# Shifting the start addresses of matmul operands inside their tiles in a hybrid mLSTM, neighbourhood and memory attention block

## The chip, the cores and the metric

The kernel runs on one core of one Trainium2 chip. The metric is the device time of one execution in microseconds (us), as the median of several runs; lower is better. Beside the runs there is one profiled execution, whose trace gives the start and length of every instruction.

## The reference

One encoder block for 512 tokens of width 1024, all in float32:

```python
h = rms_norm(x, mix_norm_g[l])
proj = h @ w_in[l]        # mLSTM q,k,v,o,gates | NA q,k,v | memory q | merge gates
y_ml = mlstm_branch(...)             # 4 heads of 128, both directions
y_na = neighbourhood_attention(...)  # 8 heads of 64 on an 8 x 64 grid
mem_k, mem_v = jnp.split(rms_norm(mem, mem_norm_g[l]) @ w_mem_kv[l], 2, axis=-1)
y_xa = memory_cross_attention(xa_q, mem_k, mem_v)   # 256 memory tokens
merged = g_ml * (y_ml @ w_br_ml[l]) + g_na * (y_na @ w_br_na[l]) + g_xa * (y_xa @ w_br_xa[l])
x = x + merged @ w_out[l]
x = x + conv_glu_ffn(rms_norm(x, ffn_norm_g[l]), ...)   # 1024 -> 2 x 2816 -> 1024
return rms_norm(x, final_norm_g)
```

Almost all of the arithmetic is in the dense projections: `w_in`, `w_mem_kv`, the three branch projections, `w_out`, and the two matrices of the feed-forward part.

## The kernel before

**Products in three parts.** To keep float32 accuracy with single-pass matmuls, both operands are split into a high part (the value rounded to the type fp32r) and a low part (what is left). The helper `mm3` (line 212) issues three matmuls for each 128-deep slice: high times high (line 213), high of the first with low of the second (line 214), low of the first with high of the second (line 215). In all of them the first operand is the stationary one, loaded into the array ahead of the matmul (a row of engine PEld, LDWEIGHTS), and the second is the moving one, which streams through it (a row of engine PE, MATMUL).

**Weights as a queue of blocks.** `block_list` writes out the order of all weight blocks, and `BLOCKS` is that order. A block's key names its kind: `mlq`, `mlk` (mLSTM queries and keys), `tm` (token-major passes: gates, values and the values of the neighbourhood attention, in three passes c = 0, 1, 2 of 272, 512 and 256 columns), `xaq`, `o`, `memk`, `memv`, `naq`, `nak`, `g` (merge gates), `br` (branch projections), `out`, `ua` and `uu` (the two halves of the feed-forward's first matrix), `dn` and `dnl` (its second matrix; `dn` has a first half, hh = 0, and a second, hh = 1; `dnl` belongs to the last two column blocks). `weights(key)` (line 201) keeps the transfers three blocks ahead (`emit_raw`, SyncE's queue, tile `wr`) and the splitting one block ahead (`emit_split`, line 176). `emit_split` cuts a block into at most two parts, and for each takes a tile `wh` (tag hi) and a tile `wl` (tag lo), each `HWT` = 576 words wide, four buffers of each: ScalarE copies the raw weights into `wh` (line 195), and VectorE subtracts to give `wl` (line 196).

**Where operands start.** A word is 4 bytes. `wh`, `wl`, the big working tiles (`unit`, 2112 words), the scratch tiles (512 words) and the raw tiles (1088 words) are all a multiple of 256 bytes long, and slices of 128, 256 or 512 words keep that phase. The constant `HI256` = 48 words (192 bytes) is the one exception of the kernel before: it shifts `wh` of the third token-major pass (lines 188 and 189), and the high part of the weights of the last column blocks, which `lastw` (line 169) keeps in four units; their low parts are not shifted.

**Which operand is which.** In projections (`proj`, line 395) the weights are stationary and the activations, 512 tokens (or 256 for the memory), are moving. In the token-major passes and for `memv` the activations are stationary and the weights moving. In `last_tiles` (line 1159) `half_tile` does the last three column blocks over the first 256 tokens, the first of them (key `dn`) over the second 256 as well, with stationary weights; after that the last two blocks are done for two groups of 128 tokens with moving weights, 256 columns.

**The attentions.** While TensorE works through projections, steps of the mLSTM and of the two attentions are put between them by generators (`step`, line 998). They share four tiles of tag R (512 words each): the rows of the mLSTM's decays (`load_R`, line 646), the queries and keys of the neighbourhood attention (`QS`, `KS`, lines 808 and 809), and queries, keys and values of the memory attention (`rt`, line 920). The neighbourhood attention's keys are the moving operand of lines 834 and 835, read as eight rows of 32 words in windows that start 0, 8, 24 or 32 words into the row (`CW`). Its gathered values lie in a unit filled by DMA (`load_vwin`, line 531) and are the stationary operand of line 872.

Of the kernel before, what the change touches and what calls it, by code (L numbers as in the profile page):

```python
# [11 lines left out]
F32 = mybir.dt.float32  # L12
F32R = mybir.dt.float32r
# [4 lines left out]
P = 128  # L18
S = 512
# [14 lines left out]
BW = 1088  # L34

GAP = 16

HI256 = 48
HWD, HWT = 544, 576
UNIT = 2112  # L40
ROWS, GW = 8, 64
# [69 lines left out]
def hybrid_block(ctx, tc, xg, xT, memT, wflat, vecs, gbias, nabias, outa, outb, outc):  # L111
# [7 lines left out]
    tp = ctx.enter_context(tc.tile_pool(name="tp", bufs=2))  # L119
# [6 lines left out]
    def nm(s):  # L126
        uid[0] += 1
        return f"{s}_{uid[0]}"

    def unit(dt=F32):  # L130
        return up.tile([P, UNIT], dt, tag="unit", name=nm("u"))
# [4 lines left out]
    def tiny(n):  # L136
        return tp.tile([P, 32], F32, tag="tiny", name=nm("y"), bufs=12)[:, :n]

    def mmps():
        return mmp.tile([P, 512], F32, tag="mm", name=nm("mm"))  # L140

# [19 lines left out]
    def halves(i):  # L161
        n, c = BLOCKS[i][1], BCOLS[BLOCKS[i][0][0]](BLOCKS[i][0])
        k = n // c
        k0 = k if n <= HWD else (k + 1) // 2
        return c, [(0, k0)] + ([(k0, k)] if k0 < k else [])

    lw = []

    def lastw(k, m):

        if not lw:
            lw.extend(unit(F32R) for _ in range(4))
        q = slice(k % 8 * 256, k % 8 * 256 + m)
        return lw[k // 8][:, HI256:][:, q], lw[2 + k // 8][:, q]

    def emit_split(i):
        key, n = BLOCKS[i]
        r = raws.pop(i)
        c, hs = halves(i)
        split[i] = []  # L180
        for a, b in hs:
            m = (b - a) * c
            if key[0] == "dnl":
                h, l = lastw(4 * key[1] + a, m)
            else:
                h = wp.tile([P, HWT], F32R, tag="hi", name=nm("wh"), bufs=4)
                l = wp.tile([P, HWT], F32R, tag="lo", name=nm("wl"), bufs=4)
                if key[:2] == ("tm", 2):
                    h = h[:, HI256:]
            for u, v in ((0, P), (P, 2 * P), (2 * P, m)) if i == 0 and a == 0 else ((0, m),):  # L190
                src = r[:, a * c + u:a * c + v]
                if i == 0 and u == 0:
                    st["wh1"] = V.tensor_copy(h[:, u:v], src).ins
                else:
                    A.activation(h[:, u:v], src, AF.Copy)  # L195
                V.tensor_tensor(l[:, u:v], src, h[:, u:v].bitcast(F32), op=ALU.subtract)  # L196
            for k in range(a, b):
                q = slice((k - a) * c, (k - a + 1) * c)
                split[i].append((h[:, q], l[:, q]))
# [17 lines left out]
    def split_act(h, l, src, scale=1.0):  # L217

        A.activation(h, src, AF.Copy, scale=scale)  # L219
        V.scalar_tensor_tensor(l, src, scale, h.bitcast(F32), op0=ALU.mult, op1=ALU.subtract)  # L220
# [48 lines left out]

    cp.tile([P, GAP], F32, name="gap")  # L270
    ident = cp.tile([P, P], F32, name="ident")
# [16 lines left out]
    for i in range(2):  # L288
        t = cp.tile([P, 514], F32, name=f"pad{i}")
# [210 lines left out]
    for c in range(3):  # L500
# [10 lines left out]
        for t in range(NT):  # L511
# [3 lines left out]
            if c < 2:  # L515
                o = 16 if c == 0 else 0
# [13 lines left out]

    def load_vwin(hp):

        vw = unit(F32R)
        for b in range(4):
            for hf in range(2):
                i = 2 * b + hf
                for r in range(4):
                    G.dma_start(vw[r * 32:(r + 1) * 32, i * 256:(i + 1) * 256],  # L538
                                nav_v[hf, r, CW[b]:CW[b] + 32, hp * 256:(hp + 1) * 256])
        return vw  # L540
# [101 lines left out]
    def ml_all():  # L642
# [3 lines left out]
        def load_R(h):  # L646
            R, rm = [], []
            for d in range(2):
                t = tp.tile([P, S], F32, tag="R", name=nm("R"), bufs=4)
                SY.dma_start(t, rd[d, h].partition_broadcast(P))  # L650
                R.append(t)
                rm.append(tp.tile([P, S], F32, tag="R", name=nm("R"), bufs=4))
            return R, rm

        def mask(R, rm):
# [105 lines left out]
        R, rm = load_R(0)  # L761
        st_h = keys(0)
        yield
        for h in range(4):
# [11 lines left out]
            for J in range(1, NT):  # L776
                E2 = weights_J(h, J, R, rm)
                if J == 3 and h < 3:
                    R, rm = load_R(h + 1)
# [14 lines left out]
    def na_all(nq, nk, vw0, yh, yl):  # L794
# [6 lines left out]
        def prep(hp):  # L801
            qn = nq[:, hp * S:(hp + 1) * S]
            kn = nk[:, hp * S:(hp + 1) * S]
            QL = QZ[hp % 2]
            QS, KS = [], []
            for e in range(2):
                own, oth = slice(64 * e, 64 * e + 64), slice(64 - 64 * e, 128 - 64 * e)
                q2 = tp.tile([P, S], F32R, tag="R", name=nm("QS"), bufs=4)
                k2 = tp.tile([P, S], F32R, tag="R", name=nm("KS"), bufs=4)
                A.activation(q2[own], qn[own], AF.Copy)  # L810
                A.activation(k2[own], kn[own], AF.Copy)
                A.activation(q2[oth], qn[own], AF.Copy)
                V.tensor_tensor(k2[oth], kn[own], k2[own].bitcast(F32), op=ALU.subtract)
                V.tensor_tensor(QL[e][own], qn[own], q2[own].bitcast(F32), op=ALU.subtract)
                QS.append(q2)
                KS.append(k2.rearrange("p (r w) -> p r w", r=ROWS))
            return QS, KS, QL
# [99 lines left out]


    def xa_all(xq, mk, mv, yh, yl):
        rt = lambda: tp.tile([P, S], F32R, tag="R", name=nm("X"), bufs=4)  # L920
        vv = lambda a: a.rearrange("p (m c) -> p m c", m=2)

        def prep(h):
            q, k = (rt(), rt()), rt()
            split_act(q[0], q[1], xq[:, h * S:(h + 1) * S])
            k = (k[:, :M], k[:, M:])
            split_act(k[0], k[1], mk[:, h * M:(h + 1) * M])
            return q, k

        def prep_v(h):  # L930
            v = rt()
            v = (v[:, :M], v[:, M:])
            split_act(vv(v[0]), vv(v[1]), vv(mv)[:, :, h * P:(h + 1) * P])
            return v

        def scores(tq, q, k):
            ps = atps()
            for i in range(2):
                t = 2 * tq + i
                tsl = slice(t * P, (t + 1) * P)  # L940
                mm3(ps[:, i * M:(i + 1) * M], q[0][:, tsl], q[1][:, tsl], k[0], k[1], True, True)
            mx = tiny(2)
            psv = ps.rearrange("p (a b) -> p a b", a=2)
            V.tensor_reduce(mx, psv, axis=AX.X, op=ALU.max, negate=True)
            V.tensor_scalar(mx, mx, XSC, None, op0=ALU.mult)
            sm = scr()
            su = tiny(2)
            for i in range(2):
                A.activation(sm[:, i * M:(i + 1) * M], psv[:, i, :], AF.Exp, scale=XSC, bias=mx[:, i:i + 1],
                             accum_out=su[:, i:i + 1])  # L950
            V.reciprocal(su, su)
            for i in range(2):
                V.tensor_scalar(sm[:, i * M:(i + 1) * M], sm[:, i * M:(i + 1) * M], su[:, i:i + 1], None, op0=ALU.mult)
            return sm

        def transposes(tq, sm, pT):
            pt = atps()
            for i in range(2):
                for hf in range(2):
                    PE.transpose(pt[:, (2 * hf + i) * P:(2 * hf + i + 1) * P],  # L960
                                 sm[:, i * M + hf * P:i * M + (hf + 1) * P], ident)
            for hf in range(2):
                ms = slice(tq * M, (tq + 1) * M)
                split_act(pT[hf][0][:, ms], pT[hf][1][:, ms], pt[:, hf * M:(hf + 1) * M])

        def values(h, v, pT):
            py = atps()
            for hf in range(2):
                vs = slice(hf * P, (hf + 1) * P)
                mm3(py, v[0][:, vs], v[1][:, vs], pT[hf][0], pT[hf][1], hf == 0, hf == 1)  # L970
            hs = slice(h * S, (h + 1) * S)
            split_act(yh[:, hs], yl[:, hs], py)

        q, k = prep(0)
        yield
        prev = None
        for h in range(4):
            sm = [scores(tq, q, k) for tq in range(2)]
            if prev:
                values(h - 1, *prev)  # L980
            yield
            v = prep_v(h)
            pT = [[sp.tile([P, S], F32R, tag="scr", name=nm("s"))[:, :S] for _ in range(2)] for _ in range(2)]
            for tq in range(2):
                transposes(tq, sm[tq], pT)
            prev = (v, pT)
            if h < 3:
                q, k = prep(h + 1)
            yield
        values(3, *prev)  # L990
        yield
# [28 lines left out]
    for f in range(4):  # L1020
# [5 lines left out]
        t = scr()  # L1026
# [262 lines left out]
    for hh in range(2):  # L1289
# [3 lines left out]
        for j in range(HF):  # L1293
            f = HF * hh + j
            if f == 0:
# [7 lines left out]
                k = KT - 1  # L1303
# [150 lines left out]
```

## Time and profile before

| | us |
|---|---|
| median of 3 runs (lowest, highest) | 879.12 (878.70, 879.23) |
| profiled execution, span from first to last instruction | 878.1 |
| TensorE matmul busy in it | 872.7 |
| TensorE weight load busy | 740.4 |
| VectorE busy | 582.2 |
| ScalarE busy | 451.4 |
| GpSimd busy | 127.1 |

The profile's page gives, for each engine, the time in which it was busy. A matmul counts as busy from its start to its modelled end, and successive matmuls overlap, so that a busy share near 100% says that there was always one under way, not how fast they follow each other. The time from one start to the next, here called the gap, is read from the timeline, or from the windows view: a stretch that begins and ends at starts of matmuls, divided by the number of gaps in it. Weight loads (PEld) run beside matmuls. The groups view lists the instructions of a line with their operands, written out<-in by the names of the tiles, their shape and count, busy time and mean length.

### The profile page before, as it was taken

To read this page: it belongs to the slowest core of one execution; us is meant where nothing else is said; L and a number is where in the kernel's file an instruction comes from. 1 tells how busy PE (TensorE), PEld (TensorE's weight loads), DVE (VectorE), ACT (ScalarE), POOL (GpSimd) and SP (SyncE) were. 2 spreads that over 40 slices of the span, in tenths; PEclk is the share of its full clock that TensorE was granted. 3 is DMA by queue.
4 is the path that set the end of the run, shared out by engine and by line. 5 is a ranking of instruction groups with operands and counts; after the bars stand their busy time and mean duration, and the time that the engine had idled before them with its cause. 6 is when DMAs were issued, how large, how long until landed. Compare 5 with 4: busy or idle time off the path is not lost.

```text
span 878.1 us, 12238 instructions
## 1 busy us (share of the span) xinstructions
PE 872.7 (99%) x4334; PEld 740.4 (84%) x4334; DVE 582.2 (66%) x1211; ACT 451.4 (51%) x953; POOL 127.1 (14%) x203
## 2 busy tenths in 40 slices
PE   9999999999999999999999999999999999999997
PEld 7898889888888888888888888888888888888897
DVE  7694686775667758898676558776633466666433
ACT  7363555754456658888544435444422344444532
POOL 0101100001072460700000002111100011111011
PEclk9999999999999999999999999999999999999999
DMA  8224643522242354533223432222233322222412
GB/s 280 99 73 140 207 135 97 192 85 90 74 137 87 107 146 131 156 110 130 97 97 109 144 107 94 99 97 96 72 103 101 109 97 97 98 97 87 141 34 96
DMA packets 39421, 99.81 MB, mean 114 GB/s; under 512 B 5688, under 2 KB 13880, under 8 KB 39360
## 3 DMA queue, kind: packets, MB, share of 16 engines
q1 hardware_dynamic: 31568, 92.32, 31.1%
q0 software_dynamic: 7360, 6.32, 3.1%
q8 instruction: 34, 0.56, 0.3%
q10 hardware_dynamic: 432, 0.39, 0.1%
q14 instruction: 27, 0.22, 0.1%
HBM read 94.80 MB, written 4.21 MB: 113 GB/s over the span
## 4 chain that ended last, share of the span: by engine, by line
PE 99%; issue 0%; ACT 0%; DVE 0%; POOLq 0%; POOL 0%; DVEq 0%
PE mm L213 29%; PE mm L215 29%; PE mm L214 29%; PE at L214 2%; PE at L213 2%; PE at L215 2%; PE at L872 1%; PE at L725 1%; PE at L853 1%; PE at L727 1%; PE at L690 1%; PE at L834 0%; PE at L835 0%; PE at L706 0%; PE at L960 0%
## 5 line engine op out<-in xcount | busy, mean ns | idle before, releaser
L213 PE MATMUL mm<-u,wh 128*128 128x512 f32 (+1 forms) x1072 | 415.6, 388 | 0.0
L215 PE MATMUL mm<-u,wl 128*128 128x512 f32 (+1 forms) x1072 | 412.2, 385 | 0.0
L214 PE MATMUL mm<-u,wh 128*128 128x512 f32 (+1 forms) x1072 | 411.8, 384 | 0.0
L195 ACT ACTIVATE wh<-wr 128x512 fp32r<-128x512 f32 (+2 forms) x298 | 184.1, 622 | 234.4 <-PE mm L214 188.1
L196 DVE TENSOR_TENSOR wl<-wr,wh 128x512 fp32r<-128x512 f32 (+3 forms) x300 | 203.1, 678 | 92.4 <-ACT wh L195 85.8
L215 PEld LDWEIGHTS mm<-u,wl 128*128 128x128 f32 x1072 | 201.5, 188 | 40.1
L214 PEld LDWEIGHTS mm<-u,wh 128*128 128x128 f32 x1072 | 201.8, 188 | 38.8
L213 PEld LDWEIGHTS mm<-u,wh 128*128 128x128 f32 x1072 | 201.8, 188 | 38.2
L1319 POOL TENSOR_TENSOR s<-s,rb 128x512 f32<-128x512 f32 x22 | 38.3, 1739 | 250.0 <-DVE s L1318 238.1
L538 POOL DMA_DIRECT2D u<-nav_d x128 | 62.2, 512 | 66.5 <-PE at L872 22.5
L219 ACT ACTIVATE u<-s 128x512 fp32r<-128x512 f32 x26 | 16.4, 630 | 57.5 <-DVE s L1322 56.1
L1322 DVE TENSOR_TENSOR s<-mm,s 128x512 f32<-128x512 f32 x22 | 15.2, 691 | 25.1 <-POOL s L1319 25.1
L458 ACT ACTIVATE s<-pad,vec 128x512 f32<-128x512 f32 x30 | 24.4, 813 | 9.5 <-DVE pad L456 9.5
L459 DVE SCALAR_TENSOR_TENSOR s<-pad,vec,s 128x512 f32<-128x512 f32 x30 | 23.6, 786 | 6.1 <-ACT s L458 6.0
L220 DVE SCALAR_TENSOR_TENSOR u<-s,u 128x512 fp32r<-128x512 f32 x26 | 18.0, 691 | 14.1 <-ACT u L219 14.0
L1318 DVE SCALAR_TENSOR_TENSOR s<-s,s 128x512 f32<-128x512 f32 x22 | 15.2, 692 | 13.4 <-ACT s L1317 13.3
L317 POOL TENSOR_TENSOR rc<-y,nhalf 128x4 f32<-128x4 f32 x1 | 1.0, 1032 | 152.9 <-DVE y L314 152.9
L460 DVE SCALAR_TENSOR_TENSOR s<-pad,vec,s 128x512 f32<-128x512 f32 x30 | 22.5, 750 | 0.7
L1317 ACT ACTIVATE s<-s 128x512 f32<-128x512 f32 x22 | 13.9, 632 | 15.1 <-DVE s L1316 15.1
L456 DVE TENSOR_TENSOR pad<-mm,rb 128x512 f32<-128x512 f32 x22 | 15.1, 691 | 7.3 <-PE mm L215 6.5
L213 PE MATMUL mm<-wh,u 128*128 128x512 f32 x48 | 18.9, 394 | 0.0
L214 PE MATMUL mm<-wl,u 128*128 128x512 f32 x48 | 18.8, 392 | 0.0
(315 smaller groups left out, 1028.4 us busy)
## 6 DMA issues: line engine op xcount, KB each, us to landing
wr<-wflat SPq DMA_DIRECT2D x141, 512.0 KB, 3.3
nab<-nabias SPq DMA_DIRECT2D x16, 256.0 KB, 2.7
u<-nav_d POOLq DMA_DIRECT2D x128, 32.0 KB, 2.6
s<-xT SPq DMA_DIRECT2D x15, 256.0 KB, 3.9
wr<-wflat SPq DMA_DIRECT2D x14, 192.0 KB, 2.3
nav_d<-nv POOLq DMA_DIRECT2D x8, 256.0 KB, 2.4
R<-rd SPq DMA_DIRECT2D x8, 256.0 KB, 3.9
wr<-wflat SPq DMA_DIRECT2D x2, 544.0 KB, 3.3
```

The lines of the kernel that those rows point to most:

```text
L195: A.activation(h[:, u:v], src, AF.Copy)
L196: V.tensor_tensor(l[:, u:v], src, h[:, u:v].bitcast(F32), op=ALU.subtract)
L213: PE.matmul(ps, lh, rh, start=start, stop=False)
L214: PE.matmul(ps, lh, rl, start=False, stop=False)
L215: st["mm"] = PE.matmul(ps, ll, rh, start=False, stop=stop).ins
L219: A.activation(h, src, AF.Copy, scale=scale)
L220: V.scalar_tensor_tensor(l, src, scale, h.bitcast(F32), op0=ALU.mult, op1=ALU.subtract)
L458: A.activation(t1, pad[:, 0:512], AF.Identity, scale=vcol(w, i), bias=vcol(b, i))
L459: V.scalar_tensor_tensor(t1, pad[:, 1:513], vcol(w, n + i), t1, op0=ALU.mult, op1=ALU.add)
L460: V.scalar_tensor_tensor(t1, pad[:, 2:514], vcol(w, 2 * n + i), t1, op0=ALU.mult, op1=ALU.add)
L538: G.dma_start(vw[r * 32:(r + 1) * 32, i * 256:(i + 1) * 256], nav_v[hf, r, CW[b]:CW[b] + 32, hp * 256:(hp + 1) * 256])
L1319: G.tensor_tensor(c, c, rb2, op=ALU.mult)
```

## The change

The weights' high and low tiles are both read and written from a start inside the tile, by kind of block: 16 words (64 bytes) for `ua`, `out`, `xaq` and `mlk`; 32 words (128 bytes) for `g`, `br`, `memv`, `naq`, all token-major passes and the second half's `dn`; 48 words (192 bytes) for `uu`, `o`, `memk` and `nak`; none for `mlq` and the first half's `dn`. The third token-major pass, where only the high part had 192 bytes, has 128 for both. The last column blocks' low parts get the 192 bytes that the high parts have. The gathered values start 192 bytes into their unit. The tag R tiles grow from 512 to 576 words, and the keys of both attentions start 64 bytes into theirs. No instruction is added or removed.

```diff
--- before.py
+++ after.py
@@ -34,8 +34,11 @@
 BW = 1088
 
 GAP = 16
+KOFF = 16
 
 HI256 = 48
+OFFSETS = {"ua": 16, "uu": 48, "g": 32, "br": 32, "out": 16, "xaq": 16, "o": 48, "memk": 48, "memv": 32,
+           "naq": 32, "nak": 48, "mlk": 16, "mlq": 0, "dn": 0}
 HWD, HWT = 544, 576
 UNIT = 2112
 ROWS, GW = 8, 64
@@ -136,6 +139,9 @@
     def tiny(n):
         return tp.tile([P, 32], F32, tag="tiny", name=nm("y"), bufs=12)[:, :n]
 
+    def rtile(dt=F32, off=0):
+        return tp.tile([P, S + 64], dt, tag="R", name=nm("R"), bufs=4)[:, off:off + S]
+
     def mmps():
         return mmp.tile([P, 512], F32, tag="mm", name=nm("mm"))
 
@@ -171,7 +177,7 @@
         if not lw:
             lw.extend(unit(F32R) for _ in range(4))
         q = slice(k % 8 * 256, k % 8 * 256 + m)
-        return lw[k // 8][:, HI256:][:, q], lw[2 + k // 8][:, q]
+        return lw[k // 8][:, HI256:][:, q], lw[2 + k // 8][:, HI256:][:, q]
 
     def emit_split(i):
         key, n = BLOCKS[i]
@@ -185,8 +191,10 @@
             else:
                 h = wp.tile([P, HWT], F32R, tag="hi", name=nm("wh"), bufs=4)
                 l = wp.tile([P, HWT], F32R, tag="lo", name=nm("wl"), bufs=4)
-                if key[:2] == ("tm", 2):
-                    h = h[:, HI256:]
+                off = 32 if key[0] == "tm" else OFFSETS[key[0]]
+                if key[:2] == ("dn", 1):
+                    off = 32
+                h, l = h[:, off:], l[:, off:]
             for u, v in ((0, P), (P, 2 * P), (2 * P, m)) if i == 0 and a == 0 else ((0, m),):
                 src = r[:, a * c + u:a * c + v]
                 if i == 0 and u == 0:
@@ -530,7 +538,7 @@
 
     def load_vwin(hp):
 
-        vw = unit(F32R)
+        vw = unit(F32R)[:, HI256:]
         for b in range(4):
             for hf in range(2):
                 i = 2 * b + hf
@@ -646,10 +654,10 @@
         def load_R(h):
             R, rm = [], []
             for d in range(2):
-                t = tp.tile([P, S], F32, tag="R", name=nm("R"), bufs=4)
+                t = rtile()
                 SY.dma_start(t, rd[d, h].partition_broadcast(P))
                 R.append(t)
-                rm.append(tp.tile([P, S], F32, tag="R", name=nm("R"), bufs=4))
+                rm.append(rtile())
             return R, rm
 
         def mask(R, rm):
@@ -805,8 +813,8 @@
             QS, KS = [], []
             for e in range(2):
                 own, oth = slice(64 * e, 64 * e + 64), slice(64 - 64 * e, 128 - 64 * e)
-                q2 = tp.tile([P, S], F32R, tag="R", name=nm("QS"), bufs=4)
-                k2 = tp.tile([P, S], F32R, tag="R", name=nm("KS"), bufs=4)
+                q2 = rtile(F32R)
+                k2 = rtile(F32R, KOFF)
                 A.activation(q2[own], qn[own], AF.Copy)
                 A.activation(k2[own], kn[own], AF.Copy)
                 A.activation(q2[oth], qn[own], AF.Copy)
@@ -917,18 +925,17 @@
 
 
     def xa_all(xq, mk, mv, yh, yl):
-        rt = lambda: tp.tile([P, S], F32R, tag="R", name=nm("X"), bufs=4)
         vv = lambda a: a.rearrange("p (m c) -> p m c", m=2)
 
         def prep(h):
-            q, k = (rt(), rt()), rt()
+            q, k = (rtile(F32R), rtile(F32R)), rtile(F32R, KOFF)
             split_act(q[0], q[1], xq[:, h * S:(h + 1) * S])
             k = (k[:, :M], k[:, M:])
             split_act(k[0], k[1], mk[:, h * M:(h + 1) * M])
             return q, k
 
         def prep_v(h):
-            v = rt()
+            v = rtile(F32R)
             v = (v[:, :M], v[:, M:])
             split_act(vv(v[0]), vv(v[1]), vv(mv)[:, :, h * P:(h + 1) * P])
             return v
```

## The prediction

> **What bounds the kernel now.** I read the page's busy times and slices first, to see whether any other engine could set the end.
>
> ```profile
> span 878.1 us, 12238 instructions
> ...
> PE 872.7 (99%) x4334; PEld 740.4 (84%) x4334; DVE 582.2 (66%) x1211; ACT 451.4 (51%) x953; POOL 127.1 (14%) x203
> ...
> PEclk9999999999999999999999999999999999999999
> ...
> PE 99%; issue 0%; ACT 0%; DVE 0%; POOLq 0%; POOL 0%; DVEq 0%
> ```
>
> The last row is from the chain of work that ended last: it is 99% TensorE. The granted clock is full throughout. So the time is the number of matmuls times the gap from one matmul's start to the next one's, and nothing else enters unless another engine runs out of slack. The next view is the groups by line with shapes kept apart, which gives the counts. Lines 213, 214 and 215 are the three matmuls of the helper `mm3`, and each has the same count, so I quote line 213's groups.
>
> ```profile
> L213 PE MATMUL mm<-u,wh 128*128 128x512 f32 x1018 | 400.0, 393 | 0.0
> ...
> L213 PE MATMUL mm<-wh,u 128*128 128x512 f32 x48 | 18.9, 394 | 0.0
> ...
> L213 PE MATMUL mm<-u,wh 128*128 128x256 f32 x54 | 15.6, 289 | 0.0
> ...
> L213 PE MATMUL mm<-u,u 128*128 128x256 f32 x44 | 13.0, 296 | 0.1
> ...
> L213 PE MATMUL at<-u,wh 128*128 128x512 f32 x14 | 5.4, 389 | 0.0
> ```
>
> The mean of 393 ns is one matmul from its start to its modelled end; they overlap, so it is no price. The price is the gap between starts. The timeline around 700 us, in the long feed-forward stage, shows it:
>
> ```profile
> 699.79 0.39 PE L213 MATMUL mm<-u,wh 128*128 128x512 f32 x1
> 700.02 0.39 PE L214 MATMUL mm<-u,wh 128*128 128x512 f32 x1
> 700.02 0.19 PEld L215 LDWEIGHTS mm<-u,wl 128*128 128x128 f32 x1
> 700.25 0.39 PE L215 MATMUL mm<-u,wl 128*128 128x512 f32 x1
> 700.25 0.19 PEld L213 LDWEIGHTS mm<-u,wh 128*128 128x128 f32 x1
> 700.47 0.39 PE L213 MATMUL mm<-u,wh 128*128 128x512 f32 x1
> ```
>
> A matmul every 0.227 us, and the weight load of the next matmul starts together with the matmul before it (both at 700.02, both at 700.25). So the two read the on-chip memory at the same time, from the same beat. The windows view makes the gap exact. Its columns are the stretch, its length, and each engine's busy time with the number of its instructions, then clock, DMA share and GB/s.
>
> ```profile
> core 0: us, PE busy (x) PEld busy (x) DVE busy (x) ACT busy (x) POOL busy (x), PEclk, DMA share, GB/s
> 527.07:846.45 319.38, 319.38 (x1411) 264.45 (x1409) 195.05 (x293) 138.21 (x223) 42.14 (x25) 1.00 0.29 98
> 49.76:61.71 11.95, 11.95 (x97) 11.95 (x96) 11.75 (x20) 6.35 (x11) 0.00 (x0) 1.00 0.25 88
> 83.52:94.83 11.31, 11.31 (x98) 11.30 (x96) 5.36 (x14) 4.76 (x10) 2.19 (x5) 1.00 0.68 218
> 846.67:850.63 3.96, 3.96 (x35) 3.95 (x33) 0.69 (x1) 1.36 (x2) 1.30 (x1) 1.00 0.02 4
> 850.63:858.40 7.77, 7.77 (x69) 7.77 (x67) 1.70 (x4) 1.86 (x4) 0.00 (x0) 1.00 0.00 0
> ```
>
> Each stretch begins and ends at a matmul's start (PE's counts take in one to three matmuls still ending at the border). First: 1409 matmuls of 512 columns, 319.38 / 1409 = 226.67 ns each. Fourth: one half tile, 11 x 3 = 33 matmuls of 256 columns, all operands at unshifted starts: 3.96 / 33 = 120.0 ns. The difference is 106.67 ns for 256 columns, so columns cost 0.4167 ns each, and both widths carry the same remainder: 226.67 - 213.33 = 13.3 and 120.0 - 106.67 = 13.3 ns. That remainder, about 6% of every wide matmul, is all that a change of start addresses could shorten.
>
> **What a start address is worth in this trace.** The kernel before already shifts some operands by 192 bytes (`HI256`), and two rows above show them. The fifth stretch is the same half tile for the next two column blocks, 2 x 11 x 3 = 66 matmuls, with the high weights (stationary, lines 213 and 214) shifted by 192 bytes and the low ones (line 215) not: 7.77 / 66 = 117.7 ns. The third stretch, from 83.52, is the third token-major pass, 96 matmuls, where the weights are the moving operand and again only the high ones are shifted (lines 213 and 215): 11.31 / 96 = 117.8 ns. Both lose 2.2 to 2.3 ns on average with two of three operands shifted, so 3.3 to 3.4 ns for each matmul whose two operands differ in phase. In the first case the stationary operand is 192 bytes ahead of the moving one, in the second 64 (modulo 256). So this trace has rows for relative shifts of 64 and 192 bytes; 128 lies between and has none. Against it: in the first token-major pass (49.76 to 61.71, 272 columns) half of the weights start 64 bytes off, because 272 columns are 1088 bytes; 11.95 / 96 = 124.5 ns, less 113.3 for the columns, leaves 11.2, only 2.1 below the usual remainder.
>
> **The change part by part.** No instruction, wait, DMA or queue entry is added, removed or moved; only start addresses change, and four buffers grow by 256 bytes each, a whole phase. ScalarE's and VectorE's copies into the shifted tiles keep shape and count; I take nothing for them. If they did slow, their cover is the slack of the rows: 195.05 and 138.21 of 319.38 us. The tightest stretch is in the attention:
>
> ```profile
> 380.00:420.00 40.00, 40.00 (x210) 34.28 (x209) 33.49 (x97) 33.82 (x88) 0.00 (x0) 1.00 0.34 116
> ```
>
> There both stand at 84 to 85%, so a TensorE faster by 1 or 2% still is what ends last.
>
> 1. Wide matmuls with a newly shifted operand. Of 1018 per line, 27 belong to `mlq` (shift 0) and 8 x 11 = 88 to the first half's `dn` (shift 0); 903 remain, with 14 more of `mlk`, and 48 with weights as the moving operand. 903 + 14 + 48 = 965 per line, 2895 in all. At 3.3 ns: **9.55 us**. Bounds: nothing, and the whole remainder, 2895 x 13.3 = 38.5 us. I take 3.3 because two independent rows give it and the remainder is equal in both widths.
> 2. Narrow ones (256 columns): 54 per line (`memk` 32, the last half tiles 22), 162, at 3.3: **0.53 us**.
> 3. Operands of already shifted groups that now shift too: the low weights of the third pass (32) and of the last tiles (44): 76 x 3.3 = **0.25 us**. The third pass's high weights go from 192 to 128 bytes; nothing.
> 4. The first pass: 96 matmuls of 272 columns, whose phases move from 0 and 64 to 128 and 192. Between 0 and the 3.3 of the others, 0.3 us; I take 0, as its remainder is already lower.
> 5. Keys and gathered values of the attentions: 64 score matmuls, 64 value matmuls and 48 of the memory attention's scores. The score rows of one step:
>
> ```profile
> 371.21 0.28 PE L834 MATMUL at<-KS,QS 128*128 128x256 f32 x1
> 371.32 0.28 PE L835 MATMUL at<-KS,QZ 128*128 128x256 f32 x1
> 371.44 0.29 PE L834 MATMUL at<-KS,QS 128*128 128x256 f32 x1
> 371.57 0.28 PE L835 MATMUL at<-KS,QZ 128*128 128x256 f32 x1
> 371.69 0.64 PE L872 MATMUL at<-w,u 128*128 128x256 f32 x4
> ```
>
> The first window of keys starts at 0 bytes and takes 0.23 us for its two, the second at 32 bytes and takes 0.25: a start can cost 10 ns a matmul too. With all 176 at 10 ns either way the bound is 1.8 us up or down; I take 0, since the windows move to 64, 96, 160 and 192, some to better and some to unknown phases.
>
> Sum: 9.55 + 0.53 + 0.25 = 10.3 us of the profiled 878.1, or 867.8. The median of the runs, 879.12, stands 1.0 above that span, so **868.8 us**. In a stage it would be a gap of 223.4 instead of 226.67 ns.
>
> **A rule that speaks against it.** The Trainium skill, "TensorE: Matmul & The Clock Gate", section "Step-by-step: what each phase is for", says that TensorE has two independent read ports and that loading the next weights takes nothing from the running matmul; its section "Wait — 56ns, not 53.3ns?" puts the fixed cost of a warm matmul at about 2.5 ns. By these the gap would be 215.8 ns at any start and the change would be worth nothing. The trace disagrees in the size, 13.3 against 2.5, and in the fifth stretch, where the shift did something.
>
> **The rivals.**
>
> *Only the load gains (no change).* In the narrow stretches the weight load is busy all the time (3.95 of 3.96 us), in the wide one only 264.45 of 319.38. If the shift shortens the load, it shows where the load sets the pace, at 256 columns, and is hidden at 512. Left are steps 2 and 3, 0.8 us: **878.3**. Against: the remainder is the same 13.3 ns in both widths, which two different causes would hardly give. (The page's rule of independent ports ends in this case too.)
>
> *Only 192 bytes help.* The kinds at 192 are `uu` (528), `o` (96) and `nak` (96), 720 wide matmuls, with `memk`'s 96 and step 3's 76: 892 x 3.3 = 2.9 us: **876.2**. For it: the first pass, where 64 bytes bought 2.1 at most, and not clearly through the start. Against: the third pass, whose relative shift is 64.
>
> *More is freed.* In the rows only two of three operands are shifted, so every change of phase inside the triple may lose something. With all three equal, half of the remainder, 6.7 ns, could go: (2895 + 162) x 6.7 = 20.5 us: **858.6**. For it: nothing but that the rows are mixed.
>
> *Slower: a bad phase.* Loads and moving reads run side by side at fixed speeds, and the start decides how often they meet. The 32-byte window of keys (0.25 against 0.23) shows that a start can be worse than 0. If 64 and 128 bytes are such phases for 512 columns, the 2895 - 720 = 2175 matmuls at those shifts lose 3.3 each, 7.2 us, and the 720 at 192 gain 2.4: 4.8 slower, **883.9**. It decides as soon as the 2175 lose over 720 x 3.3 / 2175 = 1.1 ns, a gap above 227.8 in `g`, `br`, `out` and `ua`.
>
> **How the numbers follow.** Forecast 45%; more is freed 12%; only 192 bytes 13%; no change 13%; slower 17%. Faster by over 0.2% (about what a measurement of this kernel can tell from no change, 1.8 us) is 45 + 12 + 13 = 70%, the same 13%, slower 17%. The forecast's own range is 864 to 874 (half to one and a half times the 10.3). For 8 in 10 the range reaches down to 859, which takes in most of the larger gain, and up to 880, which takes in the two small ones; the slower case and the rest of the larger one stay outside.
>
> **What would show it.** Right: in the windows over the feed-forward stage the gap of `ua`/`uu` falls from 226.67 to some 223.4, while the first half's `dn`, with shift 0, keeps 226.7; the last half tiles at 256 columns fall from 120.0 to below 117. Wrong toward no change: the 512 gaps keep 226.67 and only the 256 ones fall. Only 192: `uu` falls and `ua` does not, in alternate projections. Slower: `ua`, `g` or `br` above 227.8. ScalarE's or VectorE's mean for the split (the `wh` and `wl` groups) growing, or waits of matmuls on them, would mean that I missed a cost of the writes. The forecast is wrong altogether if the remainder of 13.3 ns has nothing to do with reads of two operands and the two shifted stretches owe their 2.3 ns to something else in which they differ, such as the tiles they sit in.

## The result, and the profile after

The changed kernel takes 893.96 us (893.74 to 894.15), the kernel before 879.17 beside it: a ratio of 1.0167, 95% interval [1.0154, 1.0181]. It is 14.8 us slower by the medians of the runs; the span of the one profiled execution of each went from 878.1 to 892.1 us.

The page of the changed kernel, the rows that answer to those of before:

```profile
span 892.1 us, 12238 instructions
...
PE 886.7 (99%) x4334; PEld 739.9 (83%) x4334; DVE 591.6 (66%) x1211; ACT 451.6 (51%) x953; POOL 123.1 (14%) x203
...
PE 99%; issue 0%; ACT 0%; DVE 0%; POOLq 0%; POOL 0%; DVEq 0%
```

The count of instructions, the chain and the clock (all slices at 9) are as they were. TensorE is still what ends last, and no wait has come in. So the same 4334 matmuls follow each other more slowly. Where, the windows view tells. First the kernel before: the first half's `dn` (264 matmuls), the second half's `ua` and `uu` (528), the second half's `dn` (165), and the half tile of 256 columns (33, shown with the prediction):

```profile
629.76:689.60 59.84, 59.84 (x266) 49.55 (x265) 21.83 (x34) 14.98 (x26) 1.79 (x1) 1.00 0.32 106
689.60:809.28 119.68, 119.68 (x530) 99.10 (x529) 80.78 (x120) 55.59 (x87) 17.99 (x10) 1.00 0.28 93
809.28:846.68 37.40, 37.40 (x167) 30.97 (x166) 17.68 (x28) 17.25 (x30) 5.68 (x4) 1.00 0.34 113
```

Then the same four stretches after the change:

```profile
639.79:699.65 59.86, 59.86 (x265) 49.55 (x264) 22.63 (x34) 14.97 (x26) 1.29 (x1) 1.00 0.34 106
699.65:822.26 122.61, 122.61 (x529) 99.23 (x528) 85.72 (x120) 55.04 (x87) 15.64 (x10) 1.00 0.28 90
822.26:860.76 38.50, 38.50 (x166) 30.97 (x165) 18.66 (x28) 17.60 (x30) 5.17 (x4) 1.00 0.33 111
860.76:864.68 3.92, 3.92 (x34) 3.92 (x33) 0.69 (x1) 1.36 (x2) 1.29 (x1) 1.00 0.02 4
```

The first `dn`, which has no shift, kept 59.84 / 264 = 226.7 ns (59.86 now). `ua` and `uu`, at 64 and 192 bytes, went from 226.7 to 122.61 / 528 = 232.2 ns. The second `dn`, at 128, went to 38.50 / 165 = 233.3. The half tile of 256 columns, also at 128, went the other way, from 120.0 to 3.92 / 33 = 118.8 ns. Adding up the gaps of all matmuls of both traces by group: 906 wide ones now at 64 bytes lost 5.9 us, 1125 at 128 lost 5.6, 720 at 192 lost 2.8, the 144 with moving weights at 128 lost 0.6. Those are the 2895 of the forecast, and they lost 14.9 us. All narrower groups together gained some 0.5, `mlq`, which has no shift, came out 0.5 lower, and the rest is small differences elsewhere: together the 14.0 us by which the span grew.

### The profile page after: what moved, and what is told of

The parts are those of the page before. It is cut to its first block, busy times and chain, and to the rows that moved or that the text cites. A ratio compares the mean times of both kernels' runs of the same rounds, so it can differ in the third digit from the quotient of the medians.

```text
span 892.1 us, 12238 instructions
## 1 busy us (share of the span) xinstructions
PE 886.7 (99%) x4334; PEld 739.9 (83%) x4334; DVE 591.6 (66%) x1211; ACT 451.6 (51%) x953; POOL 123.1 (14%) x203
## 4 chain that ended last, share of the span: by engine, by line
PE 99%; issue 0%; ACT 0%; DVE 0%; POOLq 0%; POOL 0%; DVEq 0%
PE mm L221 29%; PE mm L223 29%; PE mm L222 29%; PE at L223 2%; PE at L221 2%; PE at L222 2%; PE at L880 1%; PE at L733 1%; PE at L861 1%; PE at L698 1%; PE at L735 1%; PE at L842 0%; PE at L843 0%; PE at L714 0%; PE at L967 0%
## 5 line engine op out<-in xcount | busy, mean ns | idle before, releaser
L223 PE MATMUL mm<-u,wl 128*128 128x512 f32 (+1 forms) x1072 | 416.5, 389 | 0.0
L204 DVE TENSOR_TENSOR wl<-wr,wh 128x512 fp32r<-128x512 f32 (+3 forms) x300 | 212.9, 711 | 99.2 <-ACT wh L203 91.2
L1326 POOL TENSOR_TENSOR s<-s,rb 128x512 f32<-128x512 f32 x22 | 34.2, 1556 | 259.1 <-DVE s L1325 255.3
L1325 DVE SCALAR_TENSOR_TENSOR s<-s,s 128x512 f32<-128x512 f32 x22 | 15.2, 691 | 13.4 <-ACT s L1324 13.3
```

What stands on the lines that cost most here:

```text
L223: st["mm"] = PE.matmul(ps, ll, rh, start=False, stop=stop).ins
L1326: G.tensor_tensor(c, c, rb2, op=ALU.mult)
```

## The experiments

Two theories were left by these rows, and a third that the trace of a whole kernel can't exclude. A: with 512 columns of fp32r, TensorE alone slows as soon as its two operands differ in phase (phase here means the start modulo 256 bytes). B: a start off the 256-byte boundary is slow by itself. C: the copies of the weight split, which write at shifted starts too, get in the way of TensorE's reads.

**Cases of matmuls alone (probe1).** A kernel of nothing but matmuls on data loaded once. For each case (name, columns, start of the weights, of the moving operand, loaded columns, start of the low weights; in words) it runs

```python
CASES = [("w0", 512, 0, 0, P, 0), ("w32", 512, 8, 0, P, 8), ("w64", 512, 16, 0, P, 16), ...
for r in range(REP):
    for k in range(8):
        sl = slice(so + k * P, so + k * P + m)
        ll = slice(lo + k * P, lo + k * P + m)
        ml = slice(mo + k * 512, mo + k * 512 + n)
        PE.matmul(ps[:m, :n], WH[:, sl], XH[:, ml], start=r == k == 0, stop=False)
        PE.matmul(ps[:m, :n], WH[:, sl], XL[:, ml], start=False, stop=False)
        PE.matmul(ps[:m, :n], WL[:, ll], XH[:, ml], start=False, stop=r == REP - 1 and k == 7)
```

> Leaves out the whole computation: 25 cases of 96 matmuls each in the order of mm3, with TensorE alone at work and a pause between the cases; the cases differ in columns and in the start of the stationary and of the moving operand. Theory A (TensorE alone, relative phase): with 512 columns the gap is 226.7 ns where both operands start in the same phase (no shift, both 64, both 128), and 230 to 236 for every other shift of one of them; with 256 columns 120.0 unshifted and 115 to 119 shifted; loading fewer columns shortens the remainder of 13.3 ns in proportion. Theory B (the start as such): both 64 and both 128 are as long as one shifted alone, over 230. Theory C (the split's copies on ScalarE and VectorE meet TensorE's reads): all 512-column cases stand at 226.7 here, since nobody else is at work.

Windows over the last 63 gaps of twelve of the 25 cases, from the top: 512 columns unshifted; weights at 64, 128, 192 bytes; moving operand at 64 and 192; both operands at 64; a load of 64 columns instead of 128, unshifted; then 256 columns with weights at 0, 64, 128, 192:

```profile
22.47:36.75 14.28, 14.28 (x64) 11.82 (x63) 0.00 (x0) 0.00 (x0) 0.00 (x0) 1.00 0.01 1
...
68.81:83.51 14.70, 14.70 (x64) 11.84 (x63) 0.00 (x0) 0.00 (x0) 0.00 (x0) 1.00 0.00 0
115.72:130.42 14.70, 14.70 (x65) 11.82 (x63) 0.00 (x0) 0.00 (x0) 0.00 (x0) 1.00 0.01 1
162.42:176.84 14.42, 14.42 (x65) 11.83 (x63) 0.00 (x0) 0.00 (x0) 0.00 (x0) 1.00 0.00 0
208.83:223.25 14.42, 14.42 (x64) 11.83 (x63) 0.00 (x0) 0.00 (x0) 0.00 (x0) 1.00 0.01 1
255.27:269.97 14.70, 14.70 (x65) 11.84 (x63) 0.00 (x0) 0.00 (x0) 0.00 (x0) 1.00 0.00 0
278.51:292.79 14.28, 14.28 (x64) 11.83 (x63) 0.00 (x0) 0.00 (x0) 0.00 (x0) 1.00 0.00 1
...
347.18:361.68 14.50, 14.50 (x65) 8.45 (x63) 0.00 (x0) 0.00 (x0) 0.00 (x0) 1.00 0.00 0
...
442.87:450.43 7.56, 7.56 (x65) 7.56 (x64) 0.00 (x0) 0.00 (x0) 0.00 (x0) 1.00 0.01 2
454.99:462.13 7.14, 7.14 (x65) 7.14 (x64) 0.00 (x0) 0.00 (x0) 0.00 (x0) 1.00 0.01 2
466.84:474.31 7.47, 7.47 (x66) 7.47 (x64) 0.00 (x0) 0.00 (x0) 0.00 (x0) 1.00 0.00 0
478.99:486.41 7.42, 7.42 (x65) 7.42 (x64) 0.00 (x0) 0.00 (x0) 0.00 (x0) 1.00 0.00 0
```

VectorE, ScalarE and GpSimd stand at 0.00, and still: 14.28 / 63 = 226.7 ns unshifted, 233.3 with weights at 64 and at 128, 228.9 at 192 (14.70, 14.70 and 14.42 us). So theory C falls. Both at 64: 226.7 again, as in the case with both at 128, so B falls. A shift of the moving operand by 64 equals one of the weights by 192 (228.9), and by 192 one of the weights by 64 (233.3): what counts is the difference. (By 128 the moving operand gave 232.4, near the weights' 233.3 but not equal.) Weights at 32, 96, 160 and 224 bytes cost as much as at 64, 233.3 to 234.3. With 256 columns the order is another: 120.0 unshifted, 113.3 at 64, 118.6 at 128, 117.8 at 192.

Two more cases shift the high weights alone by 192 bytes, as the kernel before did in its last column blocks. They give 228.9 ns at 512 columns and 117.8 at 256, the same as with the low weights shifted too: the effect does not grow with the number of shifted operands. Theory A was not right in all: 228.9 and 113.3 lie outside its bounds, and loading half the columns did not shorten the wide gap but lengthened it, to 14.50 / 63 = 230.2. At 256 columns the same half load shortened it, from 120.0 to 113.3.

**Both operands at 64 bytes in the kernel (both64).**

```diff
     def unit(dt=F32):
-        return up.tile([P, UNIT], dt, tag="unit", name=nm("u"))
+        u = up.tile([P, UNIT], dt, tag="unit", name=nm("u"))
+        return u[:, KOFF:] if dt == F32R else u
...
-                h, l = h[:, off:], l[:, off:]
+                h, l = h[:, KOFF:], l[:, KOFF:]
```

The last column blocks' weights, which lie in units too, lose their 192 bytes and are at 64 with the rest.

> All high and low weights start 64 bytes into their tiles, and so do all high and low activations, so that the two operands of every wide matmul are in one phase again but off a 256-byte start. Theory A (relative phase): the gap of the feed-forward stage is 226.7 ns again and the time 878 to 880. Theory B (the start as such): the gap stays near 233 and the time is 892 to 896, since then every wide matmul has a shifted start. Theory C (writes of the split at shifted starts): as B.

It takes 879.42 us against 879.43 of the kernel before, ratio 1.0003 [0.9994, 1.0013]. The stretch of `ua` and `uu` in it:

```profile
688.85:808.53 119.68, 119.68 (x529) 99.14 (x528) 80.72 (x120) 55.59 (x87) 18.03 (x10) 1.00 0.29 93
```

119.68 us, as before to the last digit, with every start of the projections' weights and activations off the boundary. The loss came from the two operands' difference in phase, and none that can be measured from the writes at shifted starts.

**One shift for all projections (all192).**

```diff
-                off = 32 if key[0] == "tm" else OFFSETS[key[0]]
-                if key[:2] == ("dn", 1):
-                    off = 32
+                off = 32 if key[0] == "tm" else HI256
```

> Every projection's weights start 192 bytes into their tiles, with mlq and the first half's dn too; token-major passes stay at 128. Theory A: the kinds that were at 192 showed 232.2 after the change against 233.3 at 64 and 234.7 at 128, so most kinds gain 1 to 2.5 ns against the changed kernel and the 345 matmuls at shift 0 lose 5: 890 to 894. Theory of the prediction (a shift of 192 is good): below 879. If the order of shifts among neighbours sets the gap, and not the shift itself, all kinds could also come out elsewhere.

885.85 us against 879.43, ratio 1.0074 [1.0061, 1.0088]: slower than the kernel before, so 192 bytes are no good shift at 512 columns either, but less slow than expected. The same `ua` and `uu`:

```profile
694.60:815.45 120.85, 120.85 (x530) 99.23 (x528) 80.69 (x120) 55.33 (x87) 18.46 (x10) 1.00 0.29 92
```

120.85 / 528 = 228.9 ns, the value of probe1. In the changed kernel all matmuls at 192 averaged 232.2, and `uu` alone, between projections of `ua` at 64, 231.5. A kind's pace thus seems to depend on the kinds around it too; the run on neighbours below takes that up.

**Shifts only where 256 columns move (narrow).**

```diff
-                off = 32 if key[0] == "tm" else OFFSETS[key[0]]
-                if key[:2] == ("dn", 1):
-                    off = 32
-                h, l = h[:, off:], l[:, off:]
+                if key[:2] == ("tm", 2):
+                    h = h[:, HI256:]
+                elif key[0] == "memk" or key[:3] == ("dn", 1, LF - 1):
+                    h, l = h[:, HI256:], l[:, HI256:]
```

> Shifts only where 256 columns are moving: memk, the last dn block (the half tiles) and the gathered values at 192 bytes, keys of the attentions at 64; all operands of 512 columns back at phase 0; the third token-major pass and the last column blocks as in the kernel before. Theory A: the wide gap is 226.7 as before and the narrow groups keep what they gained, 0.4 us in memk, 0.2 in the half tiles and 0.2 in the attentions: 878.3 to 878.8 against 879.2. If something else in the change costs time, such as the wider R tiles or the keys, it is above 879.5.

879.03 against 879.43, ratio 0.9996 [0.9987, 1.0004], a little above the 878.3 to 878.8 expected. This is the changed kernel with the shifts of the 512-column operands undone (and those of the token-major passes and of the last blocks' low weights): the 14.8 us are gone, so the wider tag R tiles, the keys and the gathered values cost nothing that can be measured. The gain at 256 columns is too small to be told from no change.

**One kind alone (ua64).** The kernel before, with `elif key[0] == "ua": h, l = h[:, 16:], l[:, 16:]` added to `emit_split`.

> The kernel before with one part of the change alone: high and low weights of ua 64 bytes into their tiles, 528 matmuls of 512 columns. By the relative phase, with the first probe's price of 6.67 ns for each: 528 x 6.67 = 3.5 us, 882.7, and the gap in ua's projections 233.3 while uu's stay at 226.7. If the change's cost came from neighbouring kinds having different shifts or from somewhere else, less.

883.38 against 879.5, ratio 1.0047 [1.0033, 1.006]. `ua` and `uu`:

```profile
690.99:812.72 121.73, 121.73 (x529) 99.20 (x528) 80.68 (x120) 55.31 (x87) 18.07 (x10) 1.00 0.28 91
```

The stretch is 2.05 us longer than before, 7.8 ns for each of its 264 `ua` matmuls, 6.6 in `ua` itself (its gaps average 233.3). The rest is in the unshifted `uu` between, which was expected to stay at 226.7 and came to 227.8; in the case (0, 64) of the last run below, too, the groups at 0 take 227.8. The second `dn`, with 37.40 us, is untouched. The price of probe1 holds in the kernel for the shifted kind.

**Every mix of shifts at 512 columns (combos).** As probe1, with the three starts (high weights, low weights, low moving operand) each at 0, 64, 128 or 192 bytes; the high moving operand stays at 0.

> Leaves out the whole computation: TensorE alone, 64 cases of 48 matmuls of 512 columns in the order of mm3, with every mix of 0, 64, 128 and 192 bytes for the high weights, the low weights and the low moving operand (the high moving operand stays at 0). If equal phase is the best there is, no case settles below 226.7 ns. If stalls come in steps of 6.67 ns (16 columns) and can be avoided as at 256 columns (113.3 with both weights at 64 bytes in the first probe), some case settles at 220.0.

None of the 64 cases stands below the unshifted one. Over the last 24 gaps that one has 226.7; the next best (weights high 192, low 64, low moving 64) 227.8, 35 lie between 230 and 233, 20 above 233, and the worst is (64, 192, 192) at 235.6. So step 1's hope of a shorter gap at 512 columns has none among these mixes that would fulfil it.

**Widths and types (widths).**

> Leaves out the whole computation: TensorE alone, 28 cases of 72 matmuls: 512 and 256 columns in bfloat16, and 256 to 504 columns in fp32r with weights at 0, 64, 128 and 192 bytes. If the remainder belongs to reading two 4-byte operands at once, bfloat16 has a remainder well under 13.3 ns. If a phase is good or bad by where the moving operand ends, 480 and 448 columns (whose slices end 128 bytes and 0 bytes past a multiple of 256) order the shifts otherwise than 512 does; if only the start matters, they keep the order 0, 192, 64, 128.

In bfloat16, 512 columns take 215.8 ns and 256 take 109.2, a remainder of 2.5 for both, so the 13.3 belong to the 4-byte type fp32r and not to every matmul. At 480 columns unshifted weights stand at 216.7 and weights at 64, 128 and 192 bytes at 216.0, 217.8 and 218.3, at 448 columns 202.7, 202.2, 204.2 and 200.0: there the shift matters by 1 to 3 ns and in another order. Slices of 448 columns end in the same phase as those of 512, so the phase of the end does not explain the order either. At 320 columns all four stand at 146.7.

**Narrow shifts at 64 bytes (narrow64).** As narrow, with the shift that probe1 had at 113.3 ns:

```diff
-                    h = h[:, HI256:]
-                elif key[0] == "memk" or key[:3] == ("dn", 1, LF - 1):
                     h, l = h[:, HI256:], l[:, HI256:]
+                elif key[0] == "memk" or key[:3] == ("dn", 1, LF - 1):
+                    h, l = h[:, KOFF:], l[:, KOFF:]
```

Beside these lines, the last column blocks and the gathered values go to 64 bytes, the keys of the attentions back to 0, and the queries of the memory attention to 64.

> Only matmuls of 256 moving columns are shifted, and so that the stationary operand is 64 bytes ahead of the moving one, where the first probe had 113.3 ns against 120.0: memk, the last dn block and the last column blocks (high and low) at 64 bytes, gathered values at 64, queries of the memory attention at 64, and both weights of the third token-major pass, which are moving there, at 192. If the probe carries over: 96 + 66 + 64 + 48 matmuls gain up to 6.7 and 66 + 96 gain 4.4 ns, together 2.5 us, 876.6 to 877.5. If it does not: 879.

879.06 against 879.5, ratio 0.9993 [0.9985, 1.0002]: missed. The last 22 gaps of the second and of the fourth projection of `memk`, and the half tile, 33 matmuls of the last `dn`:

```profile
148.17:150.66 2.49, 2.49 (x25) 2.49 (x23) 1.58 (x4) 0.63 (x4) 0.00 (x0) 1.00 0.27 109
...
155.85:158.44 2.59, 2.59 (x25) 2.59 (x23) 1.76 (x7) 1.18 (x3) 0.79 (x1) 1.00 0.24 92
...
845.54:849.42 3.88, 3.88 (x34) 3.88 (x33) 0.69 (x1) 1.35 (x2) 1.30 (x1) 1.00 0.01 4
```

The half tile has 3.88 / 33 = 117.6 ns, not 113.3, about what 192 bytes give. `memk` has both: 2.49 / 22 = 113.2 in the second projection, as in the first and the third, and 2.59 / 22 = 117.7 in the fourth, at the same shift. So the fast pattern of probe1 does occur in the kernel, but not everywhere, and in the changed kernel, with `memk` at 192 bytes, two of its four projections had it too. Why one stretch gets it and another does not is open.

**Groups at different shifts in turn (neighbours).** As probe1, with 24 matmuls at one start and 24 at another in turn, as `ua` and `uu` alternate; and bfloat16 with shifts.

> Leaves out the whole computation: TensorE alone, 13 cases of 192 matmuls, in groups of 24 with one start of both weights for the even groups and one for the odd, as ua and uu alternate. In the changed kernel uu (192 bytes) stood at 232 ns between ua's projections (64 bytes), in the kernel with 192 everywhere at 228.9. If a projection's pace depends on what ran before it, the groups at 192 bytes stand over 229 in the case (64, 192) and at 228.9 in the case (192, 192); if only its own shift counts, at 228.9 in both. In bfloat16 (2-byte operands; remainder 2.5 ns in the run before) a shift by 64, 128 or 192 bytes costs nothing if the stalls belong to 4-byte operands, and over 2 ns if any two operands in different phases stall.

Two groups at 192 bytes of the case (64, 192), 24 gaps each, with one group at 64 before each of them:

```profile
166.47:171.98 5.51, 5.51 (x26) 4.51 (x24) 0.00 (x0) 0.00 (x0) 0.00 (x0) 1.00 0.00 0
...
177.58:183.18 5.60, 5.60 (x25) 4.54 (x24) 0.00 (x0) 0.00 (x0) 0.00 (x0) 1.00 0.02 3
```

The groups at 192 take 229.6 ns once and 233.3 the next time, at the very same addresses. In the case (192, 192) all take 228.9. So the pace is a pattern that sets in at a group's first matmuls and holds to its end, and it can only be what ran before that decides which. This fits `uu` at 192, which came to 231.5 on average beside `ua` at 64. In bfloat16 the last 143 gaps of the unshifted case:

```profile
295.61:326.47 30.86, 30.86 (x144) 14.00 (x143) 0.00 (x0) 0.00 (x0) 0.00 (x0) 1.00 0.00 1
```

That is 30.86 / 143 = 215.8 ns a gap; 64 bytes gave the same 30.86 us, and 128 and 192 bytes 215.8 ns as well.

## Why the prediction was wrong

**What bounds the kernel: right.** It is the gap of TensorE's matmuls and nothing else. No other engine came into it, and the 2895 matmuls named in step 1 are those that changed.

**Step 1 failed, in its sign.** It took 3.3 ns from stretches of 256 columns over to 512, with the argument that the remainder of 13.3 ns is the same in both. The remainder is the same, but what a shift does to it isn't: probe1, with TensorE alone, has -6.7, -1.4 and -2.2 ns at 64, 128 and 192 bytes with 256 columns, and +6.7, +6.7 and +2.2 with 512. Equal phase is the worst of the four at 256 columns and the best at 512. The size had a flaw of its own: 3.3 ns was the 2.2 of the mixed rows spread over two of three matmuls, but at 256 columns the case with the high weights alone at 192 bytes and the case with both there stand at the same 117.8. In the kernel the wide matmuls lost 14.9 us in place of the 9.55 forecast as gain: 5.1 ns each.

**Step 2 was right, step 3 was not, and both are too small to see in the time.** By the sums of the gaps `memk` gained 0.4 us and the half tiles under 0.1, of the 0.53 forecast; the first half tile fell from 120.0 to 118.8 (128 bytes), not to below 117. The third pass and the last blocks, where the low weights now shift with the high ones, lost about 0.1 us in place of the 0.25 gained. Steps 4 and 5, taken at nothing, came to 0.1 lost and 0.2 gained by the same sums.

**One of the signs was a false alarm.** The prediction named a longer mean of the split as the mark of a cost of the writes. VectorE's mean did rise, from 678 to 711 ns, but it stands at 678 in both64 and all192, where all these writes are shifted too. The last section has its cause.

**The rivals.** "A bad phase" had the cause as far as the runs show it: phases decide, and 64 and 128 are bad ones for 512 columns. Two of its sizes were off: it priced the loss at 3.3 ns, borrowed from the gain, where it was 5 to 6.7, and let 192 bytes gain, where they lose 2.2 alone and 4 between other shifts. It gave 883.9 and 17%, and the range stopped at 880. "Only the load gains" is excluded by the same rows, since the wide gaps moved. What would have helped ahead of the run: none of the rows that the prediction reads from the trace before has 512 columns in unequal phases, and step 1 bounded that unknown only on the side of gain, between nothing and the whole remainder of 13.3 ns. The key windows were a hint of a loss, though half as large as the prediction reads it: 0.25 against 0.23 us is for two matmuls, and in the trace's whole ns the pairs take 247 and 236, some 5 ns a matmul and not 10. A loss of 5 ns on 2895 matmuls is 14.5 us, or 893.6. That this comes so near to 893.96 is chance, since those rows have 256 columns, but a bound of that size on the side of loss would have been the honest one.

**The rule of the Trainium skill** ("TensorE: Matmul & The Clock Gate", "Step-by-step: what each phase is for": two independent read ports, the load takes nothing from the running matmul) agrees with the bfloat16 rows, where the gap is the same 215.8 ns at every shift. For fp32r the runs differ: the gap depends on the two operands' phases, with nothing else at work.

**What stays open** is how the phases make the stall. Averaged over a pattern, the remainders often come to multiples of 6.67 ns (6.67, 13.3, 20.0), which is 16 columns or 64 bytes of the moving operand; but a shorter load lengthened the gap at 512 columns and shortened it at 256, so a plain count of meetings between the load's reads and the moving ones does not explain it.

## What to carry to other kernels

For fp32r matmuls of 512 columns with a weight load before each, keep the stationary and the moving operand at the same start modulo 256 bytes; which start it is did not matter (0, 64 and 128 bytes for both gave 226.7), only the difference does, and it costs 1 to 9 ns of 227 per matmul over all the mixes tried. No run shifts an operand by a whole 256 bytes; that this would cost nothing rests on the kernel before, where the buffers of `wh`, 2304 bytes or nine times 256 long, all ran at 226.7. A gain measured at one width is no evidence for another. A case of a few dozen matmuls at the width in question, with no other engine at work, gave the kernel's price to within a nanosecond where one shift holds throughout (233.3 for `ua` in ua64, 228.9 in all192); with two shifts in turn it was some 2.5 ns off (`uu`: 228.9 alone, 231.5 in the kernel), and at 256 columns 4 in some stretches and nothing in others (113.3 alone, 117.6 in the half tile and 113.2 in `memk` of narrow64). In bfloat16 there was nothing to gain or lose.

## What was not expected of the hardware

A run of matmuls settles into one of several repeating patterns (for 192 bytes at 512 columns: 229.6 or 233.3 ns on average at the same addresses; for 64 bytes at 256 columns in narrow64: 113.2 or 117.7 at the same shift) and keeps it until the run ends; equal phase at 512 columns had one alone, 226.7.

VectorE's subtractions of the split rose in the changed kernel from 678 to 711 ns on average, with the longest at 1827 instead of 729, while the median stayed (686 and 685). The traces show why. Nine of the 300 take over 1700 ns, and each of them starts 10 to 98 ns behind GpSimd's multiplication `s<-s,rb`. One such meeting:

```profile
722.61 1.29 POOL L1326 TENSOR_TENSOR s<-s,rb 128x512 f32<-128x512 f32 x1 [9.31 <-DVE s L1325]
722.65 1.79 DVE L204 TENSOR_TENSOR wl<-wr,wh 128x512 fp32r<-128x512 f32 x1
```

GpSimd, which started first, has the 1.29 us that it also takes at 547.25 us of the trace before, where VectorE is idle; VectorE takes 1.79. At 701.17 us of the trace before VectorE started first, 0.04 us ahead: it took 0.69 us and GpSimd 1.80. The slower matmuls shifted the two against each other, in nine meetings so far that they changed sides. All this is off the path: the chain that ended last is 99% TensorE in both traces.
